# The low parts of every second weight granule are made by GpSimd instead of VectorE

## The chip, the cores and the metric

The kernel runs on one core of a Trainium2 chip. The metric is device time in microseconds (us) of one execution, 682.67 us as the median of two runs before the change. A core has five engines that each go through their own instructions in order and wait for each other by semaphores: TensorE (PE in the rows, with PEld for its weight loads), VectorE (DVE), ScalarE (ACT), GpSimd (POOL) and SyncE (SP), which here issues every transfer.

## The reference

Two layers of a hybrid encoder on x (512 tokens x 1024, float32), then a final RMSNorm. Each layer does:

```
h    = rmsnorm(x, norm_w)
proj = h @ w_in                      # 1024 -> 4608 columns, split into ten pieces
A: differential attention, 4 heads, two softmax maps per head, shared relative bias
B: bidirectional retention, 4 heads, rotary, decays by learned logits
C: multi-scale centred pooling, 4 groups, windows 2, 4, 8, 16, a 128x128 map per group
each times silu of its gate columns; concatenated to 1536
x    = x + mixed @ w_out             # 1536 -> 1024
```

## The kernel before

**Arithmetic.** Every float32 operand of a large product is split in two: a high part in TensorE's reduced float32 type (`fp32r`, a cast on ScalarE) and a low part, the operand minus its high part. A product is then three TensorE products (`mm3`): high x high, high x low, low x high, added up in one PSUM bank. So each weight is needed twice, as `wh` and `wl`.

**Weights.** They come as 96 granules of 128 x 1024 numbers (512 KB): 128 columns of `w_in` for a transposed projection, or 256 rows x 512 columns of `w_in` or `w_out`. `emit_granule` (line 428) loads a granule by SP into one of two raw buffers (`wraw`), and `split` (line 453) makes `wh` and `wl`, in five buffers each (`WBUFS`, line 25). The first granule comes in two halves. A unit takes its granules with `take` (line 443), which first emits granules up to five ahead. A projection unit (`proj_T`, line 515) is 24 products of 512 columns with one granule; `values` takes four granules at once, an output unit one to four (`out_half`, line 557).

**Order of work.** The units of a layer stand in `ORDERS` (line 32). The body is first only recorded. A list scheduler (`schedule`, line 201) then goes through the recorded operations with a weight for each (`cost`, line 304) and latencies between engines (line 143). At each step it takes the engine that can start first, and on it the ready operation with the lowest priority number, which is the place in the record less a boost per kind of unit (`HIGH`, line 40). That fixes the order of every engine's queue and the buffer of every tile; on the chip each engine follows its order and waits where something is late. A matmul's weight there is line 315, that of a two-input GpSimd operation line 347.

**Start of layer 0.** The first unit (`first_values`, line 702) works with granules 0 to 3 while x arrives. The token scales go out to DRAM as a row and come back spread over all partitions (`rb`, line 735), and the cosine and sine tables are multiplied by them on VectorE (`rotated`, line 773). The next three units of the order that multiply are `cg0`, `cu0` and `cu1`, with granules 4, 5 and 6.

**GpSimd before.** It does the small power operations of the norms (`square`, line 473; `headnorm`, line 549), a few memsets, and three multiplications of 512 columns at the end.

In the trace all recorded operations have one line, that of the emission (L1051), so rows are told apart by tile names: `pj`, `lg`, `tp`, `ov` are PSUM banks, `hh` and `hl` the normalised input, `wh`, `wl` and `wraw` the weights. A row of TensorE names its operands in no fixed order.

Of the kernel before, what the change touches and what calls it, by code (L numbers as in the profile page):

```python
# [15 lines left out]
P = 128  # L16
S = 512
# [11 lines left out]
HALF = (slice(0, 512), slice(512, 1024))  # L29
# Order in which the units of a layer are recorded. An output unit is named by the pairs of 128-row blocks of w_out that it takes  # L30
# (A: P Q, B: R S, C: T U) and its half of the columns.
ORDERS = [
# [5 lines left out]

# how far the units of a kind are moved ahead
HIGH = {"A": 3000, "Am": 300, "B": 3000, "t": 150, "av": -20, "qk": 60, "o": 150, "bqk": 300, "Cy": 2000, "cu": -20, "bg": -300, "cg": -20, "ag": -20}  # L40


# [1 line left out]
# The kernel body is recorded first, on tiles that have no place yet. A list scheduler then fixes the order in which  # L44
# every engine issues its instructions and the slot each tile takes, and the program is emitted in that order.

# [16 lines left out]
class View:  # L63
    """Part of a recorded tile: partitions p0..p1, free offsets idx, and the steps that lead to it."""

# [31 lines left out]
    def window(self, row, first, pattern):  # L97
        """DRAM only: elements of a row from first on, by an access pattern of its own."""
        return View(self.base, self.p0, self.p1, self.idx, self.steps + (("window", row, first, pattern),))

    def spread(self, n):
        """Every element n times, along a new last axis."""
        return View(self.base, self.p0, self.p1, np.repeat(self.idx[..., None], n, -1), self.steps + (("spread", n),))
# [47 lines left out]
class Recorder:  # L151
# [49 lines left out]
    def schedule(self):  # L201
# [39 lines left out]
        def ready(op):  # L241
            """A PSUM bank serves one engine at a time."""
            t = op.ready
            for b in op.banks:
                for e, end in b.last.items():
                    if e != op.engine:
                        t = max(t, end + latency(e, op.engine))
            return t
# [48 lines left out]

WARM = 16  # matmuls on zeros at the start
QUEUE = 8  # transfers under way in a queue
FINE = 2  # weight granules of the first columns that come in two parts  # L300
SLACK = {"PE": 0, "DVE": 80, "ACT": 40, "POOL": 0, "SP": 0}


def cost(engine, method, args, kw):
    """What an instruction weighs for the list scheduler: until its result stands, and on its engine."""
    out = args[0]
    n = out.idx.size if isinstance(out, View) else 0
    psum = any(isinstance(a, View) and a.base.space == "psum" for a in args)
    if engine == "PE":
        if method == "transpose":  # L310
            return 109, 109
        f32 = args[1].base.dt == F32 and not any(s[0] == "bitcast" for s in args[1].steps)
        if f32:
            return 2 * 110 + 4 * n * 0.417, 2 * 110 + 4 * n * 0.417
        t = max(107, n * 0.417) + 2.5
        return t, t
# [34 lines left out]
def record(ins: dict, out: bass.AP):  # L351
# [30 lines left out]

# [1 line left out]
    xt = [[sb(f"x{t}{half}", [P, 512]) for half in range(2)] for t in range(NT)]  # L384
# [14 lines left out]

# [1 line left out]
    def g_cols(l, c):  # L401
# [26 lines left out]
    def emit_granule(parts=1):  # L428
# [6 lines left out]
        for i in range(parts):  # L435
            k = slice(i * n, (i + 1) * n)
            was, nc.boost = nc.boost, HIGH.get("w", 0)
            nc.sync.dma_start(raw[:, k, :], src[:, k, :])
            split(hi[:, k, :], lo[:, k, :], raw[:, k, :])
            nc.boost = was  # L440
# [10 lines left out]

# [1 line left out]
    def split(dh, dl, src):  # L453
        nc.scalar.copy(dh, src)
        nc.vector.tensor_tensor(dl, src, dh.bitcast(F32), op=ALU.subtract)

    stats = {}

    def square(t, half, junk, part=None):
        """Mean square of token tile t: the share of one half of its columns, or of a quarter in the second half."""  # L460
        if half == 0:
# [13 lines left out]
    def scaled(t, wb, dst, half):  # L475
        """One half of the columns of the rmsnorm of token tile t."""
        c = HALF[half]
        nc.vector.scalar_tensor_tensor(dst[:, c], xt[t][half], stats[t][:, 2:3], wb[:, c], op0=ALU.mult, op1=ALU.mult)

    def transpose4(src, step=None):  # L480
        """Four 128-column blocks of src, each transposed, in one bank."""
        tp = tpp()
# [21 lines left out]
    def mm_stacked(ps, qk, m, cols):  # L504
        """Full product of slot m's query columns with its keys: both query parts lie stacked on partitions."""
        nc.tensor.matmul(ps, qk[:, m, cols], qk[:, 2 + 2 * m, :], start=True, stop=False)
        nc.tensor.matmul(ps, qk[:, m, cols], qk[:, 3 + 2 * m, :], start=False, stop=True)
# [14 lines left out]
    def stack_halves(dst, slots, src, scale, dup):  # L522
        """Split the 64 rows of each half of src. Without dup the low part goes to the other partition half of
        the same slot; with dup both parts take a slot each, present on both partition halves."""
        for m in range(2):
# [12 lines left out]
    def headnorm(ov, scale, g):  # L538
        """ov * scale * rsqrt(mean over partitions of ov^2 + eps) * g"""
        o = sb("hn", [P, UW], 1)[:, 0:S]  # L540
# [16 lines left out]
    def out_half(ms, half, after=None, before_end=None):  # L557
        """before_end: the last token tile comes in two quarters of the columns, and this follows the first."""
        ne = len(ms)
# [15 lines left out]

# [1 line left out]
    cols = sb("cols", [P, 16])  # L577
# [6 lines left out]
    def decay_tables():  # L584
        # retention decay rows: log_gamma on 8 partitions (layer, head), columns (forward, backward)
        dec = soft()[0:8, 0:16]
# [31 lines left out]

        # decay of a key to the border of its chunk that faces the other chunk, by token: columns (tile, layer, head)
        krow = soft()  # L620
# [6 lines left out]
    def column_tables():  # L627
        # per-channel columns: subln (2 rows), pool_scale (8 rows), with the gate's factor 1/2
        nc.sync.dma_start(cols[:, 0:10], ins["scales"])
# [6 lines left out]
    def bias_tables():  # L636
        # relative-position bias by distance
        oh, ohr = ttile(), ttile(dt=F32R)
# [12 lines left out]

        # lambda of each layer
        dl = soft()
# [12 lines left out]
    def toeplitz(src, row):  # L666
        """t[p, 895 - j] = value at distance j - 384 - p"""
        t = sb("wide", [P, 896], 1)
# [3 lines left out]
    def chunk_decay(row):  # L672
        """t[p, j, 255 - c] = decay at distance c - 128 j - p"""
        t = sb("wide", [P, 896], 1)[:, 0:512].rearrange("p (j c) -> p j c", j=2)
# [3 lines left out]
    def toep_tile(t, i):  # L678
        """[p, c] = value at distance c - 128 i - p"""
        return t[:, i * P:i * P + S][:, ::-1]  # L680

# [1 line left out]
    class Layer:  # L683
# [18 lines left out]
        def first_values(self):  # L702
            """Layer 0 runs on x^T w; its products take the token's rms afterwards."""
            self.vh, self.vl = sb("vh", [P, NT, 512], 1, F32R), sb("vl", [P, NT, 512], 1, F32R)
            self.rb, self.rc = sb("rb", [P, S]), edge[:, 28:32]
            # the clock of the PE array rises once it has been kept busy for a while
            dummy = sb("soft", [P, S], 4, mybir.dt.bfloat16)
# [44 lines left out]
        def scaled_T(self, ps, scale=1.0):  # L752
            """A product in its final size."""
            if self.rb is None:
# [10 lines left out]
        def gate(self, key):  # L765
            """2 silu of the next 128 gate columns."""
            ps, _ = self.scaled_T(proj_T(self.hh, self.hl))
# [5 lines left out]
        def rotated(self):  # L773
            """Next 128 columns (two heads), rotated."""
            ps = proj_T(self.hh, self.hl)
# [17 lines left out]
        def b_qk(self, pr):  # L793
            """Queries and keys of two heads; the state that each of the two chunks hands to the other one."""
            t = sb("qk", [P, 6, S], 2, F32R)
# [165 lines left out]

# [1 line left out]
    lay = Layer(0)  # L963
# [125 lines left out]
def _arrays(inputs):  # L1089
    """The inputs, some of them also in the layout that the chip wants them in, and the constants."""  # L1090
    plain = ("x", "norm_w", "w_in", "diff_lambda", "pool_w", "w_out", "rel_bias", "final_norm_w")
# [22 lines left out]
```

## Time and profile before

| | |
|---|---|
| two runs | 682.61 and 682.74 us |
| span of the profiled execution | 679.9 us |
| around it, against the median | 2.8 us |
| TensorE busy | 659.5 us (97%), 3171 products |
| VectorE busy | 500.7 us (74%) |
| ScalarE busy | 353.9 us (52%) |
| GpSimd busy | 30.3 us (4%) |
| mean granted TensorE clock | 0.994 |

The profiled execution has no total time of its own beside its span; 2.8 us is the median of the runs less the span. Products on TensorE overlap and the ends of their rows are modelled, so their starts tell the pace and not their durations.

### The profile page before, as it was taken

What the parts mean: (1) busy time and instruction counts of PE and PEld (TensorE: products, weight loads), DVE (VectorE), ACT (ScalarE), POOL (GpSimd) and SP (SyncE); (2) the same over time, 40 slices, a digit from 0 to 9 for tenths busy, and PEclk for the clock granted to TensorE, in tenths of its full rate; (3) what the DMA queues carried; (4) which work ended last, traced back from release to release, by engine and by line L of the source; (5) the groups of instructions that cost most, each with busy time, mean ns of one, the idle gap of its engine ahead of it and who ended that gap; (6) DMA issues with size and microseconds to landing.
All of it is one profiled execution on the core that took longest, in us unless ns stands there. A gap on an engine that the chain in (4) does not pass through costs nothing.

```text
span 679.9 us, 8912 instructions
## 1 busy us (share of the span) xinstructions
PE 659.5 (97%) x3171; PEld 541.1 (80%) x3171; DVE 500.7 (74%) x954; ACT 353.9 (52%) x701; POOL 30.3 (4%) x51
## 2 busy tenths in 40 slices
PE   9969999999999999999999999899999999999996
PEld 7757887878788888887888888688888887888785
DVE  5468987787787998976574779767568957887733
ACT  7525673434376866553443756344447765655321
POOL 0000000000000000001010000000000000000011
PEclk9979999999999999999999999999999999999999
DMA  9447444323326223243322423532342143224302
GB/s 325 147 127 186 139 115 117 110 94 78 90 50 181 77 91 105 69 115 91 115 63 78 139 64 88 131 118 71 95 122 65 50 150 97 71 92 90 99 31 94
DMA packets 85141, 71.86 MB, mean 106 GB/s; under 512 B 6004, under 2 KB 67604, under 8 KB 85096
## 3 DMA queue, kind: packets, MB, share of 16 engines
q1 hardware_dynamic: 85096, 71.29, 36.3%
q8 instruction: 25, 0.41, 0.2%
q14 instruction: 20, 0.16, 0.1%
HBM read 69.09 MB, written 2.18 MB: 105 GB/s over the span
## 4 chain that ended last, share of the span: by engine, by line
PE 78%; DMA 10%; DVE 6%; issue 2%; ACT 2%; SPq 1%; POOL 0%; POOLq 0%; DVEq 0%; ACTq 0%
PE pj L1051 64%; PE lg L1051 6%; PE ov L1051 4%; PE tp L1051 4%; DMA hn<-row 3%; DMA wide<-dd 2%; DVE qk L1051 1%; DMA row<-edge 1%; DVE soft L1051 1%; DMA wraw<-in_w_in 1%; DVE wl L1051 1%; DMA cols<-in_scales 1%; DMA T<-in_xT_w 1%; DMA x<-in_x 1%; ACT soft L1051 1%
## 5 line engine op out<-in xcount | busy, mean ns | idle before, releaser
L1051 PE MATMUL pj<-hh,wh 128*128 128x512 f32 x448 | 178.5, 400 | 7.9 <-ACT wh L1051 6.5
L1051 PE MATMUL pj<-hl,wh 128*128 128x512 f32 x448 | 177.5, 397 | 0.0
L1051 PE MATMUL pj<-hh,wl 128*128 128x512 f32 x448 | 176.9, 396 | 0.0
L1051 ACT CAST wh<-wraw 128x1024 fp32r<-128x1024 f32 (+1 forms) x97 | 100.8, 1039 | 106.9 <-PE pj L1051 75.8
L1051 DVE TENSOR_TENSOR wl<-wraw,wh 128x1024 fp32r<-128x1024 f32 (+1 forms) x97 | 117.3, 1210 | 29.7 <-ACT wh L1051 29.1
L1051 PEld LDWEIGHTS pj<-hh,wh 128*128 128x128 f32 x448 | 84.7, 189 | 27.1 <-ACT wh L1051 7.0
L1051 PEld LDWEIGHTS pj<-hh,wl 128*128 128x128 f32 x448 | 84.6, 189 | 18.6
L1051 PEld LDWEIGHTS pj<-hl,wh 128*128 128x128 f32 x448 | 84.7, 189 | 17.7
L1051 PE MATMUL pj<-wh,mAC 128*128 128x512 f32 (+1 forms) x264 | 87.5, 391 | 0.0
L1051 ACT ACTIVATE soft<-soft,sm 128x512 f32<-128x512 f32 x96 | 67.8, 718 | 33.9 <-DVE sm L1051 33.5
L1051 DVE TENSOR_TENSOR x<-x,pj 128x512 f32<-128x512 f32 (+1 forms) x65 | 43.6, 675 | 23.2 <-PE pj L1051 22.8
L1051 PEld LDWEIGHTS pj<-wh,mAC 128*128 128x128 f32 x264 | 49.0, 188 | 10.3
L1051 PE MATMUL lg<-qk 128*128 128x512 f32 (+1 forms) x192 | 51.4, 361 | 1.5 <-DVE soft L1051 1.5
L1051 PE MATMUL pj<-wl,mAC 128*128 128x512 f32 (+1 forms) x132 | 51.4, 389 | 0.0
L1051 POOL TENSOR_TENSOR st<-st,neghalf 128x4 f32<-128x4 f32 (+1 forms) x28 | 25.1, 896 | 477.3 <-DVE st L1051 379.2
L1051 DVE CUSTOM_DVE_ANT_0 soft<-lg,wide 128x512 f32<-128x512 f32 x64 | 43.3, 687 | 1.9 <-PE lg L1051 0.3
L1051 PE MATMUL pj<-wh,mB 128*128 128x512 f32 (+1 forms) x136 | 44.5, 383 | 0.0
L1051 PE MATMUL pj<-wh,hl 128*128 128x512 f32 x104 | 41.4, 398 | 0.0
L1051 PE MATMUL pj<-wh,hh 128*128 128x512 f32 x104 | 41.3, 398 | 0.0
L1051 PE MATMUL pj<-wl,hh 128*128 128x512 f32 x104 | 41.2, 396 | 0.0
L1051 PEld LDWEIGHTS lg<-qk 128*128 128x128 f32 x192 | 32.5, 188 | 9.6 <-DVE soft L1051 2.5
L1051 PE MATMUL ov<-T,vh 128*128 128x256 f32 x192 | 39.1, 284 | 0.4 <-DVE og L1051 0.3
(151 smaller groups left out, 949.7 us busy)
## 6 DMA issues: line engine op xcount, KB each, us to landing
wraw<-in_w_in SPq DMA_DIRECT2D x71, 512.0 KB, 4.6
wraw<-in_w_out SPq DMA_DIRECT2D x24, 512.0 KB, 4.1
hn<-row SPq DMA_DIRECT2D x16, 256.0 KB, 3.9
wide<-gd SPq DMA_DIRECT2D x8, 448.0 KB, 4.0
T<-in_xT_w SPq DMA_DIRECT2D x8, 258.0 KB, 4.1
x<-in_x SPq DMA_DIRECT2D x8, 256.0 KB, 5.0
wide<-dd SPq DMA_DIRECT2D x8, 256.0 KB, 4.8
out<-T SPq DMA_DIRECT2D x8, 256.0 KB, 2.1
```

The source lines that it names most:

```text
L1051: op.inst = getattr(getattr(tc.nc, name), method)(*[real(a) for a in op.args], **{k: real(v) for k, v in op.kw.items()})
```

## The change

Two edits touch what runs. `split` gets an optional engine for the low part, and `emit_granule` names GpSimd for granules with an odd number above 4 (5, 7, ..., 95); all others, and all other uses of `split`, stay with VectorE. And the weight of a TensorE product in the scheduler's `cost` goes from max(107, 0.417 n) + 2.5 ns to max(107, 0.4445 n + 4) ns for n columns. The rest of the diff takes comments away.

```diff
         f32 = args[1].base.dt == F32 and not any(s[0] == "bitcast" for s in args[1].steps)
         if f32:
             return 2 * 110 + 4 * n * 0.417, 2 * 110 + 4 * n * 0.417
-        t = max(107, n * 0.417) + 2.5
+        t = max(107, n * 0.4445 + 4)
         return t, t
...
             nc.sync.dma_start(raw[:, k, :], src[:, k, :])
-            split(hi[:, k, :], lo[:, k, :], raw[:, k, :])
+            split(hi[:, k, :], lo[:, k, :], raw[:, k, :], nc.gpsimd if len(wt) > 4 and len(wt) % 2 else nc.vector)
             nc.boost = was
...
-    def split(dh, dl, src):
+    def split(dh, dl, src, low=None):
         nc.scalar.copy(dh, src)
-        nc.vector.tensor_tensor(dl, src, dh.bitcast(F32), op=ALU.subtract)
+        (low or nc.vector).tensor_tensor(dl, src, dh.bitcast(F32), op=ALU.subtract)
```

## Rows read from the trace of the kernel before

**Rows 1.** The page, part 1: busy us (share of the span) x instructions.

```profile
PE 659.5 (97%) x3171; PEld 541.1 (80%) x3171; DVE 500.7 (74%) x954; ACT 353.9 (52%) x701; POOL 30.3 (4%) x51
```

**Rows 2.** Chain of waits in order of time: start us, us, what. One long piece.

```profile
352.06 37.49 PE pj L1051 x161
```

**Rows 3.** Waits of TensorE: who <- for whom: us in total, times, longest.

```profile
PE pj L1051 <- ACT wh L1051: 6.5, 1, 6.5
PE lg L1051 <- ACT T L1051: 1.6, 1, 1.6
PE lg L1051 <- DVE soft L1051: 1.5, 2, 1.2
PE pj L1051 <- DVE gate L1051: 1.3, 1, 1.3
PE tp L1051 <- ACT hn L1051: 1.2, 2, 1.0
PE tp L1051 <- DVE soft L1051: 1.2, 1, 1.2
...
```

**Rows 4.** Timeline of TensorE, 33 to 44: start us, us, what [idle before <-releaser].

```profile
33.17 0.40 PE L1051 MATMUL pj<-hh,wh 128*128 128x512 f32 x1
33.40 0.39 PE L1051 MATMUL pj<-hl,wh 128*128 128x512 f32 x1
40.33 0.80 PE L1051 MATMUL pj<-hh,wh 128*128 128x512 f32 x1 [6.54 <-ACT wh L1051]
...
43.48 0.39 PE L1051 MATMUL pj<-hl,wh 128*128 128x512 f32 x1
```

**Rows 5.** Timeline of ScalarE, the casts of granules 5 and 6.

```profile
28.36 1.04 ACT L1051 CAST wh<-wraw 128x1024 fp32r<-128x1024 f32 x1
39.23 1.04 ACT L1051 CAST wh<-wraw 128x1024 fp32r<-128x1024 f32 x1 [9.84 <-DMA wraw<-in_w_in]
```

**Rows 6.** Timeline of VectorE, 37 to 42: cosine table, low parts of granules 5 and 6.

```profile
37.70 0.69 DVE L1051 TENSOR_TENSOR cos<-cos,rb 128x512 f32<-128x512 f32 x1 [7.48 <-DMA rb<-row]
...
39.05 1.21 DVE L1051 TENSOR_TENSOR wl<-wraw,wh 128x1024 fp32r<-128x1024 f32 x1
...
40.31 1.23 DVE L1051 TENSOR_TENSOR wl<-wraw,wh 128x1024 fp32r<-128x1024 f32 x1
```

**Rows 7.** Chain of waits: the load of granule 6, from issue to landing.

```profile
32.69 6.53 DMA wraw<-in_w_in
```

**Rows 8.** Stretches (A:B us, busy by engine, PEclk, DMA): behind the long wait.

```profile
40.30:44.00 3.70, 3.67 (x10) 2.93 (x11) 3.50 (x13) 0.66 (x2) 0.00 (x0) 0.57 0.65 183
```

**Rows 9.** Groups by form: shapes xcount | busy us, mean ns | idle before.

```profile
L1051 DVE TENSOR_TENSOR wl<-wraw,wh 128x1024 fp32r<-128x1024 f32 x95 | 116.0, 1221 | 29.0 <-ACT wh L1051 28.5
...
L1051 POOL TENSOR_TENSOR soft<-x,T 128x512 f32<-128x512 f32 x3 | 3.9, 1302 | 19.9 <-DVE x L1051 13.5 <-issue 6.4
```

**Rows 10.** Stretches: length, then PE, PEld, DVE, ACT, POOL busy, PEclk, DMA.

```profile
190.00:310.00 120.00, 119.71 (x604) 99.34 (x603) 103.33 (x235) 77.77 (x165) 4.03 (x4) 1.00 0.35 98
380.00:445.00 65.00, 61.87 (x310) 50.40 (x309) 53.31 (x80) 36.77 (x64) 1.16 (x3) 1.00 0.39 100
```

**Rows 11.** Waits of SyncE's queue: the longest kind.

```profile
SPq L1051 <- DVE wl L1051: 302.6, 77, 17.0
```

**Rows 12.** Timeline of GpSimd and VectorE: a power operation at 311, one at 635.

```profile
310.85 1.22 DVE L1051 TENSOR_TENSOR wl<-wraw,wh 128x1024 fp32r<-128x1024 f32 x1
311.02 1.91 POOL L1051 TENSOR_TENSOR st<-st,neghalf 128x4 f32<-128x4 f32 x1 [11.51 <-DVE st L1051]
...
635.05 1.01 POOL L1051 TENSOR_TENSOR st<-st,neghalf 128x4 f32<-128x4 f32 x1 [12.75 <-DVE st L1051]
```

**Rows 13.** The same stretches, VectorE's low parts alone: length, busy (x count).

```profile
190.00:310.00 120.00, 20.14 (x17) 1.00 0.35 98
380.00:445.00 65.00, 11.72 (x10) 1.00 0.39 100
```

## The prediction

> **What bounds the kernel now.** The page's first part comes first: TensorE is busy 659.5 of 679.9 us and VectorE 500.7 [rows 1]. A busy TensorE may still be a waiting one, since its ends are modelled, so the chain of waits gives its true pace: one unbroken piece holds 161 products in 37.49 us, 0.233 us each [rows 2]. While that pace holds, nothing that another engine saves can show in the time. So I read next what TensorE waited for [rows 3]. The six longest kinds of wait come to 13.3 us, and one single wait of 6.5 us is half of them. Whatever this change gives has to come out of these 13.3 us (plus a slow stretch behind the long wait, below); 2% of 682.67 is 13.7 us, about what a measurement of this kernel can tell from no change.
>
> The long wait, in order. TensorE starts two products at 33.17 and 33.40 and then nothing until 40.33 [rows 4]. The two are the first of the unit that uses granule 5 (granules counted from 0); the third of that unit needs the granule's low part. ScalarE had cast the high part at 28.36 to 29.40 [rows 5], but VectorE makes the low part at 39.05 only: in its order it stands behind the product of the cosine table with the token scales, which waits 7.48 us for a transfer [rows 6]. The list scheduler must have seen no low part yet, for it put the first product of the next unit in between, and in an engine that goes in order that product holds all the rest: it needs the cast of granule 6, which runs at 39.23 to 40.27 [rows 5], because its load was issued on SP at 32.69 and took 6.53 us [rows 7]. The stall has an echo: the granted clock between 40.30 and 44.00 is 0.57 of full speed [rows 8]; the starts at 40.33 and 43.48 lie seven products apart (3.15 us, where seven at pace are 1.63) [rows 4]. The whole hole is 33.40 to 40.33 less one step, 6.70 us, and 1.52 us of slow steps: 8.2 us.
>
> **The change, part by part.**
>
> *Less on VectorE.* From the orders in the code there are 96 granules; odd ones from 5 to 95 move, 46 of them. VectorE takes 1.221 us for each [rows 9], so 46 x 1.221 = 56 us go, from 500.7 to about 445. On TensorE's path this is worth nothing by itself, since TensorE's pace covers it; it counts only where VectorE ends one of the waits in [rows 3].
>
> *More on GpSimd.* It has no row of this size. Its nearest is a two-input operation on 512 columns, 1.302 us [rows 9]. A 1024-column one lies between that (if all were fixed cost) and twice that, 2.60. I take 2.5, near the upper end, as the work doubles: 46 x 2.5 = 115 us on an engine that is otherwise nearly empty. On the path: nothing while granules are ready ahead. Five weight buffers at 24 products each (24 x 0.233 = 5.6 us) leave up to four granules, 22 us, in hand; units that take four granules at once leave one, 5.6 us, which still covers 2.5. If that cover is gone, a late low part costs up to 2.5 - 1.22 = 1.3 us each.
>
> *Granule 5 itself.* GpSimd is not behind the cosine wait. Cast done at 29.40, low part by about 32.0, before TensorE asks at 33.63. Then the planner has no reason to put the next unit in between: granule 5's unit runs 33.17 + 24 x 0.233 = 38.76. Granule 6 is still cast at 40.27, if SP keeps its order: first product at 40.33, a wait of 1.6. Its low part stays on VectorE, 40.31 to 41.54 [rows 6], so the third product, due at 40.80, waits another 0.8. New hole 2.4 us; the clock should hold, as it does between 380 and 445, where TensorE's idle time (65.00 - 61.87 = 3.1 us) goes with a granted clock of 1.00 [rows 10]. **Gain: 8.2 - 2.4 = 5.8 us.**
>
> *Queues passed.* SP's wait for a raw buffer, released until now by VectorE's low part, comes to 302.6 us over 77 waits [rows 11]; 46 releases now come from GpSimd, about 1.3 us later each. Behind them in SP's order stand the small transfers of the head normalisation. With two raw buffers a granule needs about 6.5 (longest load) + 1.0 + 2.5 = 10 us of one, so 5 us per granule, against 5.6 at pace: covered, narrowly. In GpSimd's queue the small power operations (1.01 us [rows 12]) can now stand behind a 2.5 us subtraction. Bounds 0 and 2.5 us each for the sixteen; I take 0, since TensorE has other units to run meanwhile.
>
> *The planner's weight of a product.* The diff also raises it, for 512 columns, from 216.0 to 231.6 ns, almost exactly the measured 233. No instruction changes, the orders of all queues may. Nothing in the trace prices that; bounded by the other waits of [rows 3], 6.8 us won if all go, 6.8 lost if they double. I take 0, as a plan nearer to the pace has no sign.
>
> *Do GpSimd and VectorE disturb each other?* One direction stands in the trace: the same power operation takes 1.91 us at 311.02 and 1.01 at 635.05; in the first case VectorE's 1.22 us subtraction of two SBUF tiles had begun at 310.85 [rows 12]. It ends at 312.07, GpSimd 0.86 later. The other direction, VectorE held by a long GpSimd operation, has no row: the bounds are 0 and the whole 2.5 us for each of 46. I take 0 on TensorE's path. The Trainium skill ("SBUF — State Buffer", section "Who interferes with whom") says that a VectorE instruction with two SBUF inputs and a GpSimd instruction that reads SBUF exclude each other, and that the later one fully blocks. The 1.91 agrees for one direction; by that rule the second direction holds too, and the relief of 56 us turns into up to 115 us of standing.
>
> Sum: 679.9 - 5.8 = 674.1 of span; around the span lie 682.67 - 679.9 = 2.8 us, so 676.9. I say **677**.
>
> **Rivals.**
>
> *VectorE held by GpSimd, where VectorE is tight.* From 190 to 310 it is busy 103.3 of 120 us, from 380 to 445 53.3 of 65 [rows 10], with 17 and 10 low parts in them [rows 13]. Half of these 27, 13.5, move: 16.5 us saved, 33.8 us held. If VectorE stands through all of that, its net loss is 13.5 x 1.28 = 17 us, and with no cover 682.7 - 5.8 + 17 = **694**. Against it: even then VectorE fits (103.3 + 8.5 x 1.28 = 114 of 120). For it: chains there pass between VectorE and ScalarE by small steps, and some TensorE waits already end on VectorE. The point at which the change loses: 5.8 / 1.28 = 5 of the 46 uncovered; over 2% slower from (13.7 + 5.8) / 1.28 = 15. It need not be complete; half of it is 685. The rule of the skill's SBUF page would bring this case. Chance 0.22, of which 0.06 beyond 2%.
>
> *The first hole stays.* The new order could still put a product that needs granule 6 early, or SP's order could move granule 6's load back. For it: every order is planned anew, and the plan thinks the transfer behind the cosine wait far quicker than it is. Against it: nothing in granule 5's own path waits any more. Time: unchanged, **682**. Chance 0.12.
>
> *The later waits go as well.* Half of the low parts off VectorE, and a plan at the right pace, could take the 6.8 us of the other five kinds: 676.9 - 6.8 = **670**; with the remaining 2.4 us too, 668. For it: three of the five end on VectorE (1.5, 1.3 and 1.2 us). Against it: the other two end on ScalarE, which gets no relief [rows 3]. Chance 0.13, of which 0.06 beyond 2%.
>
> **Numbers.** The forecast itself has 0.53, at 677 and by itself between 674 and 681. The range 671 to 688 takes it in with the first hole staying, half of the contention case and half of the last: about 0.8. Faster by over 2% 0.06, slower by over 2% 0.06, within 2% 0.88.
>
> **What would show it.** TensorE's gap at 33 us shrinks to about 1.6 and 0.8, and the clock row holds 1.00 there; GpSimd's low part of granule 5 begins near 29.5; GpSimd's subtractions take about 2.5 us, VectorE has 46 fewer. The contention case shows as idle time of VectorE, or stretched two-input operations, beside GpSimd's, with TensorE waiting for VectorE between 190 and 445. I am wrong if the hole is as before, if new waits of TensorE behind GpSimd appear, or if the pace of 0.233 changes.

## The result and the profile after

737.91 us, median of two runs (737.56 and 738.27), against 682.67: a ratio of 1.0825, 95% interval [1.0794, 1.0856]. The change costs 55 us; the prediction said 677.

The page of the kernel after, its first line, part 1, and the two groups of part 5 that make the low parts (shapes xcount | busy us, mean ns | idle before, releaser):

```profile
span 735.8 us, 8932 instructions
PE 681.3 (93%) x3171; PEld 544.6 (74%) x3171; DVE 496.3 (67%) x908; ACT 353.3 (48%) x701; POOL 141.5 (19%) x97
...
L1051 POOL TENSOR_TENSOR wl<-wraw,wh 128x1024 fp32r<-128x1024 f32 x46 | 113.6, 2470 | 341.6 <-ACT wh L1051 303.8 <-PE tp L1051 19.7 <-issue 17.4
...
L1051 DVE TENSOR_TENSOR wl<-wraw,wh 128x1024 fp32r<-128x1024 f32 (+1 forms) x51 | 65.9, 1291 | 36.2 <-ACT wh L1051 36.1
```

46 low parts moved and take 2.470 us each. But VectorE, with 46 instructions fewer, is busy 496.3 us and not the 445 that the move should leave [rows 1]. The 445 is a little low, since neighbouring rows of VectorE overlap by some 0.08 us: e7 below drops the same 46 and is left with 453.0. Some 43 us have come back on it. TensorE has the same 3171 products in 55.9 us more of span. Its waits, longest kinds first (who <- for whom: us in total, times, longest):

```profile
PE tp L1051 <- DVE soft L1051: 6.8, 6, 1.9
PE pj L1051 <- DVE u L1051: 6.7, 1, 6.7
PE tp L1051 <- ACT hn L1051: 5.6, 5, 2.8
PE pj L1051 <- DVE soft L1051: 4.8, 5, 1.9
PE lg L1051 <- ACT T L1051: 3.9, 2, 2.2
...
PE ov L1051 <- DVE T L1051: 2.2, 2, 1.9
```

There are 19 kinds with 47.9 us in 41 waits, against 8 kinds with 14.2 us in 10 before [rows 3]. The 6.5 us for granule 6's cast is gone; most of the new ones end on VectorE or on what follows from it, and several stop at 1.9 to 2.8 us. The pace itself has not moved: a chain piece of the kernel after has 49 products in 11.36 us, 0.232 us each. Behind stalls the clock falls. Stretches of the kernel after (A:B, length, busy of PE, PEld, DVE, ACT, POOL, then granted clock and DMA), two of the seven at half clock, and the one that answers to [rows 10]:

```profile
51.50:61.70 10.20, 6.17 (x14) 4.63 (x15) 9.44 (x14) 3.67 (x4) 2.51 (x3) 0.50 0.72 169
89.00:92.40 3.40, 3.40 (x17) 3.21 (x16) 2.03 (x4) 2.56 (x6) 0.00 (x0) 0.51 0.79 194
...
190.00:310.00 120.00, 113.34 (x542) 90.58 (x542) 94.69 (x218) 71.59 (x151) 22.95 (x11) 0.99 0.28 81
```

Six stretches of 3.4 us at half speed lose about 1.7 us each, the long one half of TensorE's 6.17 busy us: some 13 us, against 1.5 before. With 47.9 - 14.2 = 33.7 us of waits that is 45 of the 55 us; the rest lies in pauses too short for the list. Between 190 and 310 TensorE gets 542 products through where it got 604.

Where this time of VectorE's went is seen beside GpSimd. Timelines of the kernel after, first GpSimd, then VectorE, at four places (start us, us, what):

```profile
42.57 2.39 POOL L1051 TENSOR_TENSOR wl<-wraw,wh 128x1024 fp32r<-128x1024 f32 x1 [12.91 <-ACT wh L1051]
...
55.35 2.37 POOL L1051 TENSOR_TENSOR wl<-wraw,wh 128x1024 fp32r<-128x1024 f32 x1 [0.50 <-ACT wh L1051]
...
259.50 2.65 POOL L1051 TENSOR_TENSOR wl<-wraw,wh 128x1024 fp32r<-128x1024 f32 x1 [13.98 <-PE tp L1051]
...
281.30 2.44 POOL L1051 TENSOR_TENSOR wl<-wraw,wh 128x1024 fp32r<-128x1024 f32 x1 [8.92 <-ACT wh L1051]
```

```profile
42.31 0.16 DVE L1051 TENSOR_SCALAR soft<-soft 8x2 f32<-8x2 f32 x1
42.50 0.15 DVE L1051 TENSOR_TENSOR soft<-soft 8x2 f32<-8x2 f32 x1
42.68 2.29 DVE L1051 TENSOR_SCALAR soft<-soft 8x2 f32<-8x2 f32 x1
...
55.83 2.44 DVE L1051 TENSOR_TENSOR mAC<-hn,mAC 128x512 fp32r<-128x512 f32 x1 [0.45 <-ACT mAC L1051]
...
259.82 2.36 DVE L1051 TENSOR_TENSOR sm<-sm,cols 128x1 f32<-128x1 f32 x1
262.10 0.68 DVE L1051 SCALAR_TENSOR_TENSOR soft<-pj,rb 128x512 f32<-128x512 f32 x1
...
281.53 0.68 DVE L1051 CUSTOM_DVE_ANT_0 soft<-lg,wide 128x512 f32<-128x512 f32 x1
282.14 0.08 DVE L1051 DVE_READ_ACCUMULATOR2_ANT sm<- 128x1 f32 x1
282.14 0.69 DVE L1051 TENSOR_TENSOR T<-tp,T 128x512 fp32r<-128x512 f32 x1
```

A 0.16 us operation with one input of 8x2 numbers takes 2.29 us and ends at 44.97, when GpSimd's subtraction ends (42.57 + 2.39 = 44.96). At 259.82 one on 128x1 numbers takes 2.36 us and ends at 262.18, GpSimd at 262.15. At 281 to 283 two instructions that take one input from PSUM (`lg`, `tp`) run in their usual 0.68 and 0.69 us within a subtraction. Each VectorE instruction set against the median of its own operation, tiles and shape in the trace of before, 30 of them are over 0.2 us longer, 45.3 us together: 26 with two inputs in SBUF (`sm<-sm,cols` six times), four casts or scalings with one, and none with an input from PSUM, while 29 of the latter began and ended inside a subtraction unhindered. So what stands is above all an instruction with two SBUF inputs, whatever its size, for what is left of GpSimd's. With one SBUF input both happen: beside the four that stood, 13 on 128x1 or 128x2 numbers ran through inside a subtraction. Below, this excess over the usual time is called the *stretch*.

How a held instruction reaches TensorE is seen behind the one at 259.82. Timelines of the kernel after, ScalarE, then TensorE:

```profile
262.27 0.72 ACT L1051 ACTIVATE soft<-soft,sm 128x512 f32<-128x512 f32 x1 [2.17 <-DVE sm L1051]
...
264.18 0.63 PE L1051 MATMUL tp<-ident,soft 128*128 128x128 f32 x4 [1.92 <-DVE soft L1051]
```

ScalarE stood 2.17 us for the held `sm`, and TensorE 1.92 us for the `soft` that VectorE made out of ScalarE's result.

Last, the step for which I had a gain. Timeline of TensorE in the kernel after (idle before <-releaser in brackets):

```profile
39.11 0.40 PE L1051 MATMUL pj<-hh,wl 128*128 128x512 f32 x1
41.01 0.50 PE L1051 MATMUL pj<-hh,wh 128*128 128x512 f32 x1 [1.50 <-DVE soft L1051]
41.35 0.39 PE L1051 MATMUL pj<-hl,wh 128*128 128x512 f32 x1
42.27 0.51 PE L1051 MATMUL pj<-hh,wl 128*128 128x512 f32 x1 [0.53 <-DVE soft L1051]
...
48.41 0.40 PE L1051 MATMUL pj<-hl,wh 128*128 128x512 f32 x1
55.53 0.76 PE L1051 MATMUL pj<-hh,wh 128*128 128x512 f32 x1 [6.72 <-DVE u L1051]
```

The hole of [rows 4] has become 41.01 - 39.11 - 0.23 = 1.67 and 42.27 - 41.35 - 0.23 = 0.69 us: 2.36, forecast 2.4. At 48.41 a new one begins, of 6.9 us, for VectorE's `u<-pj,rb`, which frees a PSUM bank.

### The profile page after: what moved, and what is told of

Same layout as the page of the kernel before. It is cut to its first block, busy times and chain, and to the rows that moved or that the text cites. A ratio compares the mean times of both kernels' runs of the same rounds, so it can differ in the third digit from the quotient of the medians.

```text
span 735.8 us, 8932 instructions
## 1 busy us (share of the span) xinstructions
PE 681.3 (93%) x3171; PEld 544.6 (74%) x3171; DVE 496.3 (67%) x908; ACT 353.3 (48%) x701; POOL 141.5 (19%) x97
## 5 line engine op out<-in xcount | busy, mean ns | idle before, releaser
L1051 PE MATMUL pj<-hh,wh 128*128 128x512 f32 x448 | 181.4, 406 | 13.1 <-DVE u L1051 6.7
L1051 PE MATMUL pj<-hh,wl 128*128 128x512 f32 x448 | 179.4, 403 | 0.5 <-DVE soft L1051 0.5
L1051 POOL TENSOR_TENSOR wl<-wraw,wh 128x1024 fp32r<-128x1024 f32 x46 | 113.6, 2470 | 341.6 <-ACT wh L1051 303.8
L1051 PEld LDWEIGHTS pj<-hh,wl 128*128 128x128 f32 x448 | 86.1, 192 | 20.2 <-DVE soft L1051 1.0
L1051 PEld LDWEIGHTS pj<-hl,wh 128*128 128x128 f32 x448 | 86.4, 193 | 18.3
L1051 DVE TENSOR_TENSOR wl<-wraw,wh 128x1024 fp32r<-128x1024 f32 (+1 forms) x51 | 65.9, 1291 | 36.2 <-ACT wh L1051 36.1
L1051 POOL TENSOR_TENSOR st<-st,neghalf 128x4 f32<-128x4 f32 (+1 forms) x28 | 22.8, 815 | 194.8 <-DVE st L1051 160.6
```

Source lines behind the costliest of these rows:

```text
L1051: op.inst = getattr(getattr(tc.nc, name), method)(*[real(a) for a in op.args], **{k: real(v) for k, v in op.kw.items()})
```

## The experiments

My theories ahead of them: **1**, GpSimd's subtractions hold VectorE (the rival that I had given 0.22); **2**, the planner's new weight made a worse plan; others came up on the way and stand in the expectations. All ratios are to the kernel before on the same chip in the same batch.

| run | median us | ratio [95%] |
|---|---|---|
| e1 weight alone | 697.63 | 1.0219 [1.0197, 1.0241] |
| e2 move alone, planned | 708.26 | 1.0379 [1.0358, 1.0401] |
| e3 move alone, order of before | 709.26 | 1.0383 [1.0355, 1.0411] |
| e4 plan of after, all on VectorE | 716.03 | 1.0477 [1.0448, 1.0506] |
| e5 extra subtractions | 738.75 | 1.0816 [1.0781, 1.0850] |
| e6 extra fills | 707.50 | 1.0354 [1.0301, 1.0407] |
| e7 fills in place of low parts | 682.34 | 0.9980 [0.9958, 1.0001] |
| e8 the same, raw buffer held | 682.48 | 1.0004 [0.9975, 1.0032] |
| e9 high minus high | 695.00 | 1.0179 [1.0138, 1.0221] |
| e10 granule 5 alone, planned | 687.05 | 1.0065 [1.0038, 1.0092] |
| e11 start only, in place | 681.55 | 0.9978 [0.9957, 0.9999] |
| e12 weight 202 | 682.42 | 0.9995 [0.9970, 1.0021] |
| e13 weight 224 | 689.67 | 1.0101 [1.0065, 1.0137] |
| e14 subtractions in quarters | 708.47 | 1.0372 [1.0335, 1.0409] |
| e15 start, scales on another queue | 681.01 | 0.9977 [0.9959, 0.9994] |
| e16 move, weight 202 | 703.39 | 1.0315 [1.0284, 1.0346] |
| e17 start, load ahead of the scales | 682.94 | 1.0000 [0.9984, 1.0017] |

### The change taken apart

**e1**: the second edit alone.

```diff
-        t = max(107, n * 0.417) + 2.5
+        t = max(107, n * 0.4445 + 4)
```

> The kernel before with one edit, the planner's weight of a TensorE product (216.0 to 231.6 ns for 512 columns); all low parts on VectorE. Theory 1 (GpSimd's subtractions hold VectorE's two-input instructions, and the held VectorE stops TensorE): 675 to 692, little changed. Theory 2 (the newly planned orders do the damage, whoever makes the low parts): 720 to 740. Theory 3 (a low part that comes 1.25 us later stops TensorE directly): 675 to 692.

**e2**: the kernel after with the old line for the weight.

> The changed kernel with the planner's old weight of a TensorE product; the 46 low parts on GpSimd, planned there. Theory 1: 720 to 745, most of the loss remains, with some 45 us by which VectorE's instructions are stretched. Theory 2: 675 to 692. Theory 3: 720 to 745, with TensorE's waits ending on GpSimd's low parts.

**e3**: every queue in the order of before, only the engine of the 46 swapped at emission.

```diff
+            if op.odd:
+                name = "gpsimd"
```

> The kernel before with its planned order of every engine kept; only the engine that issues the 46 low parts is GpSimd at emission, the planner still thinks VectorE. Nothing is planned anew. Theory 1: 710 to 745. Theory 2: 675 to 685. Theory 3: 710 to 745, with TensorE's waits ending on GpSimd.

**e4**: the other way round, the plan of the kernel after with `name = "vector"` for the 46.

> The changed kernel with its planned order of every engine kept, as if the 46 low parts ran on GpSimd; at emission VectorE issues them, at the place in its queue that the plan's times give. No long GpSimd operation is left, VectorE has 56 us more. Theory 1: 680 to 700. Theory 2: 720 to 740 or more. Theory 3: 680 to 700.

The weight alone costs 15 us, the move alone 25; together 55, so 14 to 15 more than the sum. My ranges knew only one cause or the other: e1 lies above the 692 of theory 1 and below the 720 of theory 2, e2 and e3 below the 720 and 710 of theory 1. The move costs the same whether planned anew or put into the old order (e2, e3): the 25 us are not the planner's doing. Their trace shows theory 1: stretches of 46.1 us in 32 instructions in e3 and the same in e2, none in e1 and e4. Theory 3, TensorE waiting for the later low parts themselves, falls: no wait of TensorE's products in e2, e3, e9 or the kernel after ends on GpSimd. e4 went past my 680 to 700: I put that down to a plan that leaves VectorE 56 us too little room, and so it says nothing about the weight by itself; e1 does.

**e12, e13, e16**: the weight of a 512-column product at 202 and at 224 ns (216 before, 231.6 after) in the kernel before, and at 202 in the kernel after.

```diff
-        t = max(107, n * 0.417) + 2.5
+        t = max(107, n * 0.389) + 2.5
```

> The kernel before with the planner's weight of a 512-column product lowered from 216 to 202 ns, further from the chip's 232. Theory 5 (a plan that thinks TensorE too fast puts more products between dependent steps, and this slack is what the heavier weight took away): 676 to 686. Theory 6 (the units' orders are fitted to one weight, and any other loses): 690 to 705.

> The same weight at 224 ns, half way to the changed kernel's 231.6, which took 15 us more. Theory 5: 685 to 694, between the two. Theory 6: 690 to 705, with no order by weight.

> The changed kernel with the planner's weight of a 512-column product at 202 ns in place of 231.6 (the old weight, 216, gave 708 with the same move). Theory 5 (slack in the plan covers lateness, that from held VectorE too): 695 to 707. If slack does not help against the hold: 707 to 715.

202, 216, 224 and 231.6 ns give 682.4, 683, 689.7 and 697.6 us; beside the move 202, 216 and 231.6 give 703.4, 708.3 and 737.9. Nothing is gained below 216 without the move, and every step up costs. I read it so: a plan that thinks TensorE quicker than its 233 ns puts more products between steps that depend on each other; the error was slack, and the truer weight takes it out. The order of the times fits that; the slack itself is in no row here, and of e1's 15 us TensorE's listed waits hold only 5.4 (19.6 against 14.2). That the orders of before merely happened to fit is not borne out: 202 is another plan and as fast. That the price compounds because a held VectorE needs that slack is likewise argued: beside the move 202 gains 5 us over 216, without it nothing.

### What in the move costs

**e7, e8**: order of before; GpSimd fills the 46 low parts with zeros (left out: the subtraction), so it reads nothing and VectorE is still relieved; in e8 further fills were to keep the raw buffer as long as the subtraction would.

```diff
+            if op.odd:
+                low, raw, high = (real(a) for a in op.args)
+                tc.nc.gpsimd.memset(low.bitcast(F32), 0.0)
+                continue
```

> As the swap in place (the planned order of before kept), but GpSimd only fills the 46 odd low parts with zeros: it reads nothing, so the raw buffer is free after ScalarE's cast, and the low part stands about 1 us after the cast. Left out: the low parts of these granules. Neither a reading GpSimd operation nor a late buffer. Theory 1 (a reading GpSimd operation holds VectorE) and theory 4 (the raw buffer is given back later, and the next load with it): both 672 to 686, so that the relief of VectorE by itself shows. If it is over 695, any move off VectorE costs, and both fall.

> As the filling kernel, and behind each filled low part GpSimd also fills the raw buffer one and a half times, so the raw buffer is held some 2.4 us after the cast, as the subtraction holds it, with no reading by GpSimd. Left out: the same low parts. Theory 1: 674 to 688, as without the hold. Theory 4: 698 to 712.

VectorE falls to 453.0 us busy in e7 and the time stays where it was: the relief is worth nothing, as forecast. The stretch in e7 is 1.4 us: a GpSimd that only writes hardly holds VectorE. But e8 does not test a later release, as I had meant it to. The fill of the low part does not wait for the cast and mostly ran ahead of it, so the raw buffer is released 2.04 us behind the end of the cast in the mean of the 46, and no later than before (2.44).

**e9**: GpSimd subtracts the high part from itself (its low parts are zeros; the raw buffer is not read).

```diff
+                tc.nc.gpsimd.tensor_tensor(low, high, high, op=ALU.subtract)
+                continue
```

> As the swap in place, but GpSimd subtracts the high part from itself: as long and as much reading as the true subtraction, the low part as late, but the raw buffer is not read, so it is free after ScalarE's cast. Left out: the low parts of the 46 odd granules (they come out zero). Theory 1: 695 to 712, with VectorE stretched by some 45 us. Theory 4: 674 to 688.

Group by form of e9, GpSimd's subtractions (columns as above):

```profile
L1055 POOL TENSOR_TENSOR wl<-wh 128x1024 fp32r<-128x1024 f32 x46 | 89.3, 1942 | 341.3 <-ACT wh L1057 305.5 <-DVE sm L1057 14.1 <-DVE qk L1057 11.4
```

As soon as GpSimd reads SBUF, the stretch is back (31.1 us in 29) and 12 us with it. e3 has 46.1 us of stretch and costs 26. The difference of 14 is not settled: subtractions of 2.46 instead of 1.94 us, more of them in a bad place, or the raw buffer's release, 2.79 us behind the cast in e3 and at the cast itself in e9.

**e5, e6**: everything as before, and GpSimd works besides it, behind each of the 46 low parts of VectorE: one subtraction into the raw buffer, no longer needed then (e5), or two fills of it (e6).

```diff
+            if op.odd:
+                raw, high = real(op.args[1]), real(op.args[2])
+                tc.nc.gpsimd.tensor_tensor(raw, raw, high, op=ALU.subtract)
```

> The kernel before, order and all, with VectorE still making all low parts; behind each of the 46 odd granules' low parts GpSimd does one more subtraction of the same size (raw buffer minus high part, written over the raw buffer, which nobody reads any more). TensorE waits for none of these; a raw buffer is held some 2.5 us longer. Theory 1: VectorE stretched by 40 to 60 us, time 710 to 745. Theory 2: 680 to 690. Theory 3: 680 to 690 (no low part is later than before, only loads).

> As the one before, but GpSimd fills the dead raw buffer with zeros twice instead of subtracting: it writes and reads nothing, and holds the raw buffer about as long. Theory 1 in the form that GpSimd's reading is what holds VectorE: VectorE hardly stretched, 682 to 690. If any long GpSimd operation holds VectorE, or if the later release of the raw buffer is the cause: as slow as the subtraction beside.

VectorE's busy time in e5 is 559.1 us against 500.7, with the same 954 instructions; the stretch is 60.1 us in 35. Two groups by form tell the two engines' part, of e5:

```profile
L1056 POOL TENSOR_TENSOR wraw<-wraw,wh 128x1024 f32<-128x1024 f32 x46 | 116.0, 2522 | 397.9 <-DVE wl L1053 240.4 <-issue 43.3 <-DVE sm L1053 31.1
...
L1053 DVE TENSOR_TENSOR wl<-wraw,wh 128x1024 fp32r<-128x1024 f32 x95 | 125.0, 1316 | 33.1 <-ACT wh L1053 32.8
```

e6 was to come out near 682 to 690 and came out at 707.5 with a stretch of 3.0 us. So e5 was not the clean test that I took it for: both keep the raw buffer 1.9 to 2.5 us beyond VectorE's low part, and I put e6's 24 us down to that (its casts wait 41.9 us for loads of `w_in`, 28.9 before). What e5 costs above e6, 31 us, I put down to VectorE being held. In the changed kernel the buffer is not kept that long, since GpSimd begins right behind the cast: it is released 2.63 us behind it in the mean, against 2.44 before and 4.51 in e6.

**e14**: e3 with each subtraction in four of 256 columns.

```diff
+                low, raw, high = (real(a).rearrange("p k c -> p (k c)") for a in op.args)
+                for i in range(0, 1024, 256):
+                    tc.nc.gpsimd.tensor_tensor(low[:, i:i + 256], raw[:, i:i + 256], high[:, i:i + 256], op=ALU.subtract)
```

> The swap in place, but each of the 46 subtractions on GpSimd comes in four of 256 columns. If VectorE is held for one whole GpSimd instruction and gets its turn between them, each hold is at most about 0.7 us and VectorE is stretched by well under the 46 us of the whole ones: 685 to 700. If the hold lasts as long as GpSimd has such work, or four starts cost as much: 705 to 715.

Group by form of e14:

```profile
L1056 POOL TENSOR_TENSOR wl<-wraw,wh 128x256 fp32r<-128x256 f32 x184 | 155.4, 875 | 323.5 <-ACT wh L1058 302.8 <-PE lg L1058 10.0 <-DVE og L1058 7.6
```

Shorter pieces let VectorE in between: the stretch falls to 26.2 us in 58, about 0.45 us each. But a granule now takes GpSimd 155.4 / 46 = 3.4 us, the raw buffer is released that much later, and the time is the same. So the stretch alone does not tell the time. Beside the mean release of the 46 raw buffers behind the end of their casts:

| run | stretch, us | release, us | cost, us |
|---|---|---|---|
| before | 0 | 2.44 | 0 |
| e7 | 1.4 | at the cast | 0 |
| e8 | 2.9 | 2.04 | 0 |
| e9 | 31.1 | at the cast | 12 |
| e3 | 46.1 | 2.79 | 26 |
| e14 | 26.2 | 3.70 | 25 |
| e6 | 3.0 | 4.51 | 24 |
| e5 | 60.1 | 5.12 | 55 |

An estimate by two terms: e9 gives 0.39 us for each us of stretch, e6 then 11 us for each us by which the mean release is later than before. That makes 22, 24 and 53 us for e3, e14 and e5, where 26, 25 and 55 were measured. By it 18 of e3's 26 us are the stretch. No run separates the two within the move, and which instruction stands may count too.

### The hole at the start

**e10**: granule 5 alone on GpSimd, planned anew with the old weight.

```diff
+            split(hi[:, k, :], lo[:, k, :], raw[:, k, :], nc.gpsimd if len(wt) == 5 else nc.vector)
```

> The planner's old weight, and granule 5's low part alone made by GpSimd, planned there. The prediction's step for itself: TensorE's hole at 33 us shrinks to 1.6 and 0.8 us, time 676 to 680. If VectorE's late start (it waits for the token scales until 38 us) gives it back at 48 us by a wait for a PSUM bank: 680 to 690. Theory 2 (whatever is planned anew loses): 690 to 700.

The hole falls to 2.16 + 0.69 us, and waits of 1.68 us at 50.9, 1.43 at 59.9 and 2.83 at 174 come up: 4.4 us slower. One moved instruction gives a plan with other waits.

**e11, e15, e17**: order of before, granules 5 and 6 on GpSimd right behind their casts. In e11 SP issues granule 6's load ahead of `rb`; in e15 besides, the scales' small transfer (`row`, 2 KB) goes out on ScalarE's queue; in e17 SP issues the load ahead of both. The edit of e17:

```diff
+        for op in moved:
+            cast = next(o for o in order if o.engine == "ACT" and o.args[0].base is op.args[2].base)
+            order.remove(op)
+            order.insert(order.index(cast) + 1, op)
...
+        order.remove(row)
+        order.remove(rb)
+        order[order.index(load) + 1:order.index(load) + 1] = [row, rb]
```

> The planned order of before kept, with three moves at the start: the low parts of granules 5 and 6 go to GpSimd, right behind their casts, and SP issues granule 6's load ahead of the load that waits for the token scales. No low part then stands behind the cosine product and granule 6 is not late, so TensorE's hole of 6.7 us at 33 us should close. If the 8.2 us stay won: 674 to 678. If VectorE, which still starts its backlog only when the token scales land at 38 us, holds the PSUM banks and gives it back by new waits between 44 and 60: 679 to 684.

> As the start kernel, and the small transfer of the token scales to DRAM is issued by ScalarE and not by SP, because granule 6's load, issued at 27.0 ahead of the waiting one, still landed only at 39.5, with the DMA engines at 0.02 of their time between 27 and 30. If it was the scales' transfer that held those behind it on the same queue: the load lands near 32, TensorE's hole at 33 closes to under 2 us. Time then 674 to 678 if the 8 us stay won; 679 to 684 if VectorE's late start gives them back. If the load lands at 39 again: 680 to 684 with the hole as before.

> The kernel before, in its own order, with two edits at the start: the low parts of granules 5 and 6 are made on GpSimd right behind their casts, and SyncE issues granule 6's load ahead of the scales' small transfer (row) and of rb, which waits for it. Theory A, the scales' small transfer holds every load behind it until it is through: granule 6's load now lands near 32 us instead of 38 to 40, TensorE's hole at 33 us closes to under 2 us, and the 6 to 7 us either stay won (674 to 678 us) or go back at about 48 us, because VectorE gets rb some 2 us later and frees PSUM late (679 to 684 us). Theory B, the load is late for another reason (its buffer, or the DMA engines' own order): it still lands after 38 us, the hole stays over 5 us, time 681 to 684 us.

In e11 the load was issued at 27.01, 5.7 us earlier than in [rows 7], and landed at 39.53, as late as before; the hole stayed at 6.6 us. Stretch 27 to 30 of e11 (length, busy by engine, clock, DMA share, GB/s):

```profile
27.00:30.00 3.00, 3.00 (x14) 2.42 (x14) 2.59 (x10) 2.81 (x5) 0.11 (x1) 1.00 0.02 5
```

It moves 5 GB/s while a 512 KB load is due. e15 says the same from another queue (issued 27.96, landed 40.01). In e17, issued at 26.20 ahead of the small transfer, it was there at 29.97 for the cast, and the hole at 33 is gone altogether. The time is that of before. The chain of waits of e17 (start us, us, what) and its TensorE waits in the timeline:

```profile
26.63 9.38 DMA row<-edge
36.04 0.03 issue
36.07 5.98 DMA rb<-row
42.08 0.69 DVE cos L1067
```

```profile
46.12 0.76 PE L1067 MATMUL pj<-hh,wh 128*128 128x512 f32 x1 [1.99 <-ACT wh L1067]
48.49 0.80 PE L1067 MATMUL pj<-hh,wl 128*128 128x512 f32 x1 [1.17 <-DVE wl L1067]
55.41 0.47 PE L1067 MATMUL pj<-hh,wh 128*128 128x512 f32 x1 [1.59 <-DVE u L1067]
```

The scales now come 4.4 us later to VectorE (cosine product at 42.08, 37.70 in [rows 6]), and TensorE pays at 46 to 56 with 4.75 us of waits and a granted clock of 0.52 from 46 to 52. Theory A holds, in its second branch: the small transfer holds the loads behind it, and the gain goes back at 46 to 56. That the hole was slack for a VectorE that starts late, and not TensorE's loss alone, fits this, e10 and the kernel after; e17 by itself does not show it, since its own order brings the scales later.

## Why the prediction was wrong

**"I take 0 on TensorE's path"** (GpSimd and VectorE disturbing each other) failed first. I had the rule and one row of it, 1.91 us at 311 [rows 12], and the upper bound of 2.5 us; by e3 the move costs 26 us with nothing else changed, by e9 12 where GpSimd reads and keeps no raw buffer, by e7 nothing where it does not read. So 12 of the 26 are shown to be the reading; how the rest divides between it and the raw buffer's release only the estimate above tells. Two things hid it. I priced the rival through VectorE's busy share in two tight stretches and found that it "fits", but a chain such as `sm` between two ScalarE steps is on TensorE's path even where VectorE has time to spare: the 128x1 operation of 2.36 us became 1.92 us of TensorE's. And I looked only from 190 to 445, while 46 low parts lie over the whole span. So the rival was mis-sized too: 694 is 11 us over before, and e3 alone is 26 over. By the Trainium skill ("SBUF — State Buffer", section "Who interferes with whom") a VectorE instruction with two SBUF inputs and a GpSimd one that reads SBUF exclude each other, and one that only writes does not count. The traces agree in both halves: 46.1 us of stretch in e3, 1.4 in e7. That rule forecast more than the row I leaned on.

**"I take 0, as a plan nearer to the pace has no sign"** failed next. It has a sign: 15 us alone (e1), outside the bounds of 6.8 that I took from the waits of before, because a new plan makes waits that the old trace does not hold; and 29.6 beside the move (708.3 to 737.9). e12 and e13 show the direction; why the truer weight is worse is argued, not shown.

**"Gain: 8.2 - 2.4 = 5.8 us"** was right where I looked (2.36 us) and worth nothing: it came back at 48 us in the kernel after, as new waits in e10, and in e17, where the hole closes fully, at 46 to 56. I had not asked what VectorE owes at that point: it is late by the scales' transfers, and the PSUM banks that it frees are due next (`u<-pj,rb` at 48 us).

What held: 46 moved at 2.470 us (forecast 2.5); VectorE's relief worth nothing (e7), though its busy time fell by 48 us and not 56; no wait of TensorE's products for GpSimd's low parts; the pace, 0.232 us; granule 5's low part off the cosine wait. "Covered, narrowly" for the raw buffers is not shown: they are released 0.2 us later in the mean, and e6 says that 2 us there cost 24. Chances: 0.06 for slower by over 2% was far too little for two costs, each without a row, that I had set to 0 one after the other though both could only be bounded.

No run beat the kernel before by more than 0.23%; e15 and e11 are the nearest, at 681.

## What to carry to other kernels

Before an elementwise operation on SBUF is moved to GpSimd, count the VectorE instructions with two inputs in SBUF that would run beside it, the tiny ones in dependent chains above all: here such an instruction stood for the whole rest of GpSimd's, and the relief of VectorE paid nothing back. Ask also when the move gives a staging buffer back. A wrong weight in a planner may be slack that the plan lives on; a truer one is a change of its own, to be timed alone. Before a hole is counted as a gain, ask whether the engine that is due behind it is ready earlier too.

## What the runs showed of the hardware

- The transfer of 2 KB to DRAM takes 8.3 us from issue to landing in the kernel before and 9.4 in e17, where a 512 KB load is ahead of it. The load issued behind it, on its queue (e11) or another (e15), takes some 12 us and hardly moves at first: 0.02 of the DMA engines' time, 5 GB/s in e11. Ahead of it the load takes under 4 (e17).
- GpSimd's fill of 128x1024 takes 0.954 us, its subtraction with one input read twice 1.942, with two inputs 2.46 to 2.52 (e6, e9, e3, e5).
- The run that keeps one of two raw buffers 1.9 us beyond VectorE's low part is 24 us slower (e6).
- Beside a GpSimd subtraction of 2.4 to 2.65 us, VectorE instructions on 8x2 and 128x1 numbers took 2.29 and 2.36 us instead of 0.16, those with an input from PSUM their usual time (the kernel after).
